# The inverse root of a recurrence's norm: from ScalarE's Sqrt to Newton steps on VectorE

## The chip, the cores and the metric

The kernel runs on one core of one Trainium2 chip. The core has five engines, each of which executes its own instructions in order: TensorE (PE in the profile), VectorE (DVE), ScalarE (ACT), GpSimd (POOL) and SyncE (SP), which here issues nearly all DMAs. They wait for each other by semaphores. The metric is the device time of one execution in microseconds (us): the median of several runs. One execution more is taken by the hardware profiler.

## What is computed

One decoder block over 1024 tokens of width 1024, all in float32. What matters here is the first half, the mixer:

```python
proj = x @ w_in                      # q | f | i | o_gate | pool_v | gate_a | gate_b
f = lb + (1 - lb) * sigmoid(f_pre);  k = 1 - f
o = hgrn2_chunked(silu(q) * 128 ** -0.5, k, i_val, log(f))   # 8 heads, state 128 x 128
o = o * lax.rsqrt(jnp.mean(jnp.square(o), axis=-1, keepdims=True) + RMS_EPS)
o = o * hgrn_norm_g * sigmoid(o_gate)
merged = sigmoid(gate_a) * (o @ w_a) + sigmoid(gate_b) * pooled_branch
mix = merged @ w_out
```

After it come two layer norms and a squared-ReLU MLP (1024 to 4096 to 1024). The line with rsqrt, the inverse root of each head's mean square, is what the change touches.

## The kernel before

Precision. Products of float32 are made of three passes: both operands are split into a high part (a cast on ScalarE, line 118 for weights, line 123 for activations) and a low part (a subtraction on VectorE, lines 119 and 124), and TensorE multiplies high by high, high by low and low by high (lines 201, 203, 204 in prod; 105 to 107 in mm3). The big products go by a seven-product scheme over 2 x 2 blocks: the function pair makes one such set for 256 columns of a weight, with sums of weight blocks on VectorE (lines 241, 284, 289), copies out of PSUM on ScalarE (271) and sums out of PSUM on VectorE (275).

Stages. First the transposes of x and the values i; then the heads, about 150 to 600 us of the span; then the products with w_a, with w_out, the first norm, the MLP and the last norm. Only the heads matter below.

The heads. A loop over eight heads h and two halves u of 512 tokens calls hgrn(h, u), sixteen times in all. It works on one head's 128 channels as 128 x 512 tiles, and each call in this order:

- VectorE scans the products of f (811), ScalarE makes k = 1 - f (813), VectorE takes four reciprocals of 128 columns (817), GpSimd makes small decay tables (819 to 838), VectorE and ScalarE make the scaled queries and keys (841 to 865);
- TensorE transposes the scaled keys, ke (870), ScalarE copies them into the tile tH (872), TensorE multiplies them with the values (875), and VectorE carries the state st over four chunks of 128 tokens (880, 883);
- TensorE makes the scores in the PSUM tile sc (887, 898), and VectorE copies them under the causal mask into the tile att (905), of which there is one only;
- TensorE makes the output o in PSUM, four chunks of one or two matmuls (915, 918);
- ScalarE squares o and sums along each row into ss, 128 x 4 (923); then comes the inverse root (924, 925); then ScalarE copies o, scaled by it, into tH (928), which has one buffer and is thus the tile that the next call's keys will need;
- TensorE transposes it (931), VectorE multiplies with the gain and the output gate in the tile og, two buffers (932), and SyncE stores the row to DRAM (933).

Between the calls stand products that do not depend on the recurrence: the next head's q and f (head_inputs), output gates, the pooling branch (pooled), the gates a and b (gates), and near the end pool_products, which loads rows back into the tiles og and v and splits them for TensorE. o_sums(kp) loads four stored rows of the recurrence back from DRAM, forms sums for the w_a products on VectorE (608 to 611) and stores them (613).

Order. The program is written in the order of the loops, but the framework schedules it: it simulates the program with its own durations, takes for each engine the next instruction that its model has ready, earlier-written ones first, and writes down the order that results. On the chip each engine keeps to that order. A change in one place can so move instructions on all engines. Tiles come from pools with a fixed number of buffers, and a new tile waits until the old use of its buffer is over.

ScalarE's functions sit in tables. Square, Copy, Identity and Sigmoid go with the table that the heads use, Sqrt is in another: in each call line 924 is preceded by a table load, and the next Sigmoid (lines 653, 660, 679, 696) by one back.

Of the kernel before, what the change touches and what calls it, by code (L numbers as in the profile page):

```python
# [9 lines left out]
F32 = mybir.dt.float32  # L10
F32R = mybir.dt.float32r
U32 = mybir.dt.uint32
AF = mybir.ActivationFunctionType
ALU = mybir.AluOpType

_TC = dict(schedule_with_timeline_sim=True)
P = 128
# [6 lines left out]
CH = HALF // P  # L24
# [12 lines left out]
LN_EPS = 1e-5  # L37
RMS_EPS = 1e-6
QSCALE = float(P) ** -0.5
PSUM = bass.MemoryType.PSUM  # L40


@with_exitstack
def tile_hybrid_block(
# [19 lines left out]
    V, A, G, PE = nc.vector, nc.scalar, nc.gpsimd, nc.tensor  # L64
# [5 lines left out]
    const = ctx.enter_context(tc.tile_pool(name="const", bufs=1))  # L70
    pp = ctx.enter_context(tc.tile_pool(name="pp", bufs=4, space=PSUM))
    hd = ctx.enter_context(tc.tile_pool(name="hd", bufs=1, space=bass.MemoryType.DRAM))
# [8 lines left out]
    def nm(s):  # L81
        seq[0] += 1
        return f"{s}_{seq[0]}"
# [48 lines left out]
        out=cmask, in_=cmask, compare_op=ALU.is_ge, fill=0.0, base=0,  # L132
        pattern=[[1, P]], channel_multiplier=-1,
    )
    eps_rms = const.tile([P, 1], F32, name="eps_rms")
    G.memset(eps_rms, RMS_EPS)
    eps_ln = const.tile([P, 1], F32, name="eps_ln")
    G.memset(eps_ln, LN_EPS)
    inv_n = const.tile([P, HALO], F32, name="inv_n")
# [120 lines left out]
    def c_late():  # L260
        return c_tile(False)
# [140 lines left out]
    with tc.tile_pool(name="xr", bufs=8, side="right", reuse_waits="tile") as xr:  # L402
# [17 lines left out]
        V.tensor_sub(e01[:, 8:16], prm[:, 8:16], lb)  # L420
        A.activation(e01, e01, AF.Exp)
        V.tensor_add(lb, e01[:, 0:8], e01[:, 8:16])
# [169 lines left out]
    def loaded(src, tile_of):  # L592
        t = tile_of()
        nc.sync.dma_start(out=t, in_=src)
        return t
# [22 lines left out]
    with tc.tile_pool(name="tmp", bufs=1, side="right", reuse_waits="tile") as tmp:  # L618
# [14 lines left out]
        def tt(tag, dtype=F32):  # L633
            pool = tmp if tag in ("q", "f", "og", "v") else hgp
            return pool.tile([P, HALF], dtype, tag=tag, name=nm(tag), bufs=RINGS.get(tag, 1))

        def small(tag, shape, bufs=2):
            n = math.prod(shape[1:])
            t = hgp.tile([P, max(n, LINE)], F32, tag=tag, name=nm(tag), bufs=bufs)[:, :n]
            return t if len(shape) == 2 else t.rearrange("p (a b) -> p a b", b=shape[2])  # L640


        def head_inputs(h, behind=()):
# [6 lines left out]
            def take_f(u):  # L650
                def take(src):
                    t = fs[u] = fs[u] or tt("f")
                    A.activation(t, src, AF.Sigmoid)
                    A.activation(t, t, AF.Identity, bias=lb[:, h : h + 1], scale=one_lb[:, h : h + 1])
                return take

            def take_q(u):
                def take(src):
                    t = qs[u] = tt("q")
                    A.activation(t, src, AF.Sigmoid)  # L660
                    V.scalar_tensor_tensor(t, src, QSCALE, t, ALU.mult, ALU.mult)
                return take
# [11 lines left out]
        def output_gates(h):  # L674

            def take(dst, src=False):
                def put(t):
                    s = c_late() if src else t
                    A.activation(s, t, AF.Sigmoid)
                    nc.sync.dma_start(out=dst, in_=s)  # L680
# [7 lines left out]
        def gates(j):  # L688
# [3 lines left out]
            def take(dst, src=None, more=None):  # L692
                def put(t):
                    s = (tt("v") if spare else c_late()) if src else t
                    more_of = loaded(more, lambda: tt("v")) if more is not None else None
                    A.activation(s, t, AF.Sigmoid)
                    if more_of is not None:
# [34 lines left out]
        def pooled(g):  # L732
# [58 lines left out]
                (lambda: room(0, 0), lambda: room(0, 1), lambda: room(1, 1)), (take_11, take_12, take_21, lambda _: None),  # L791
            ))

        def blk(t):
            return t.rearrange("p (b s) -> p b s", s=SUB)

# [9 lines left out]
        def hgrn(h, u, ft, q, v, og, state):  # L806
# [8 lines left out]
            for i in range(CH):  # L815
                w = slice(i * P, (i + 1) * P)
                V.reciprocal(r[:, w], fd[:, w])  # L817
            T = small("T", [P, NB])
            G.tensor_copy(T, blk(fd)[:, :, SUB - 1])
            T2 = T.rearrange("p (b e) -> p b e", e=2)  # L820
            p32 = small("p32", [P, CH, 4])
# [21 lines left out]
            V.tensor_mul(kc, k, r)  # L843
            kr = tt("tE")
            V.tensor_mul(blk(kr), blk(kc), bc(T, [P, NB, SUB]))
            A.copy(pairs_of(kc)[:, :, 0], pairs_of(kr)[:, :, 0])
            qc = tt("tF")
# [49 lines left out]
            for c in range(CH):  # L897
# [7 lines left out]
            V.copy_predicated(  # L905
                at, cmask.bitcast(U32).unsqueeze(1).to_broadcast([P, CH, P]),
                sc.rearrange("p (c t) -> p c t", t=P),
# [11 lines left out]
            ss = small("ss", [P, CH])  # L919
            on = tt("tH")  # L920
            for c in range(CH):
                w = slice(c * P, (c + 1) * P)
                A.activation(on[:, w], o[:, w], AF.Square, accum_out=ss[:, c : c + 1])
            A.activation(ss, ss, AF.Sqrt, bias=eps_rms, scale=1.0 / P)
            V.reciprocal(ss, ss)
            for c in range(CH):
                w = slice(c * P, (c + 1) * P)
                A.activation(on[:, w], o[:, w], AF.Copy, scale=ss[:, c : c + 1])
# [18 lines left out]
        for h in range(HEADS):  # L947
            fs, qs = nxt
            state = None
            for u in range(2):  # L950
                v, og = values(h, u), loaded(ogd[h][u], lambda: tt("og"))
                with tc.high_priority(PRIO_LAST) if (h, u) == (HEADS - 1, 1) else nullcontext():
                    state = hgrn(h, u, fs[u], qs[u], v, og, state)
                    if (h, u) == (HEADS - 1, 1):
                        tags = iter(("tD", "tE", "tF", "tC"))
                        o_sums(h - CH, lambda: tt(next(tags)))
                if h + 1 < HEADS and u:
                    nxt = head_inputs(h + 1)
                    if h % 2:
                        output_gates(h + 1)  # L960
                for what, j in EXTRAS.get((h, u), ()):
                    dict(gates=gates, pooled=pooled, pool_products=pool_products, o_sums=o_sums)[what](j)
# [439 lines left out]
```

## Time and profile before

| | us |
|---|---|
| median of 3 runs | 1464.81 |
| lowest and highest run | 1462.62 to 1467.08 |
| the profiled execution, its own time | 1460.19 |
| its span, first to last instruction | 1458.5 |
| TensorE idle within the span | 22.1 |
| of it between 550 and 600 us | 6.75 |
| mean granted clock of TensorE | 0.996 |

How the views are read. A group row reads: line, engine, operation, output tile <- input tiles, shapes, count | busy time, mean duration in ns of one | idle time of the engine just before them, and what ended it. A timeline row reads: start, duration, engine, line, operation, tiles, count, and in brackets the idle time before it with what released it. A row of the view by stretch reads: from and to, then the length of the stretch and the busy time with counts for PE, PEld (weight loads), DVE, ACT and POOL, the granted clock, the busy share of the DMA engines and what they moved. A DMA row gives size and the median time from issue to landing. Numbers of buffers are left out of the names.

### The profile page before, as it was taken

To read this page: it belongs to the slowest core of one execution; us is meant where nothing else is said; L and a number is where in the kernel's file an instruction comes from. 1 tells how busy PE (TensorE), PEld (TensorE's weight loads), DVE (VectorE), ACT (ScalarE), POOL (GpSimd) and SP (SyncE) were. 2 spreads that over 40 slices of the span, in tenths; PEclk is the share of its full clock that TensorE was granted. 3 is DMA by queue.
4 is the path that set the end of the run, shared out by engine and by line. 5 is a ranking of instruction groups with operands and counts; after the bars stand their busy time and mean duration, and the time that the engine had idled before them with its cause. 6 is when DMAs were issued, how large, how long until landed. Compare 5 with 4: busy or idle time off the path is not lost.

```text
span 1458.5 us, 20662 instructions
## 1 busy us (share of the span) xinstructions
PE 1436.4 (98%) x7377; PEld 1187.9 (81%) x7377; DVE 1141.6 (78%) x1838; ACT 758.3 (52%) x1383; POOL 58.6 (4%) x244
## 2 busy tenths in 40 slices
PE   8999999999999998999999999999999999999997
PEld 7888888888888886788888878888888888888886
DVE  5967989899898885768985597666666787777977
ACT  5445565666656655556542376555555443333535
POOL 0001001001000010000002100000000100000000
PEclk9999999999999999999999999999999999999999
DMA  7232233323234447897672225444474874445322
GB/s 253 70 126 87 85 98 101 109 75 114 90 99 138 152 132 249 301 299 241 223 247 99 73 94 195 159 146 144 152 261 149 275 260 150 153 141 163 130 73 116
DMA packets 160615, 226.82 MB, mean 156 GB/s; under 512 B 11232, under 2 KB 84480, under 8 KB 160512
## 3 DMA queue, kind: packets, MB, share of 16 engines
q1 hardware_dynamic: 158576, 218.93, 44.7%
q0 software_dynamic: 1152, 4.19, 0.8%
q10 hardware_dynamic: 784, 2.38, 0.5%
q8 instruction: 58, 0.95, 0.3%
q14 instruction: 45, 0.37, 0.1%
HBM read 154.16 MB, written 71.30 MB: 155 GB/s over the span
## 4 chain that ended last, share of the span: by engine, by line
PE 94%; DVE 3%; DMA 1%; ACT 1%; issue 0%; SPq 0%; DVEq 0%
PE ps_pj L201 16%; PE ps_pj L203 16%; PE ps_pj L204 16%; PE ps_pj L1283 4%; PE ps_pj L1285 4%; PE ps_pj L1284 4%; PE ps_pj L106 3%; PE ps_pj L107 3%; PE ps_pj L105 2%; PE ps_tr L1285 1%; PE ps_tr L1283 1%; PE ps_tr L1284 1%; PE ps_sc L201 1%; PE ps_sc L203 1%; PE ps_sc L204 1%; PE ps_hg L203 1%
## 5 line engine op out<-in xcount | busy, mean ns | idle before, releaser
L201 PE MATMUL ps_pj<-act,w 128*128 128x512 f32 x1068 | 421.6, 395 | 0.4 <-ACT act L123 0.2
L203 PE MATMUL ps_pj<-act,w 128*128 128x512 f32 x1068 | 415.1, 390 | 0.5 <-DVE act L124 0.5
L204 PE MATMUL ps_pj<-act,w 128*128 128x512 f32 x1068 | 414.1, 390 | 0.0
L201 PEld LDWEIGHTS ps_pj<-act,w 128*128 128x128 f32 x1068 | 200.6, 188 | 42.8 <-ACT act L123 0.6
L204 PEld LDWEIGHTS ps_pj<-act,w 128*128 128x128 f32 x1068 | 200.5, 188 | 42.3
L203 PEld LDWEIGHTS ps_pj<-act,w 128*128 128x128 f32 x1068 | 200.6, 188 | 40.6 <-DVE act L124 0.9
L118 ACT CAST w<-t 128x512 fp32r<-128x512 f32 x170 | 104.7, 620 | 105.0 <-PE ps_pj L203 53.8
L118 ACT CAST w<-raw 128x512 fp32r<-128x512 f32 x143 | 88.2, 620 | 117.3 <-PE ps_pj L203 62.5
L119 DVE TENSOR_TENSOR w<-raw,w 128x512 fp32r<-128x512 f32 x143 | 99.8, 702 | 55.2 <-ACT w L118 53.9
L119 DVE TENSOR_TENSOR w<-t,w 128x512 fp32r<-128x512 f32 x170 | 115.9, 685 | 29.6 <-ACT w L118 29.4
L1245 ACT CAST act<-act 128x1024 fp32r<-128x1024 f32 x66 | 66.9, 1050 | 107.9 <-issue 35.0
L1246 DVE TENSOR_TENSOR act<-act,act 128x1024 fp32r<-128x1024 f32 x66 | 79.3, 1220 | 18.5 <-ACT act L1245 15.8
L1285 PE MATMUL ps_pj<-act,act 128*128 128x512 f32 x240 | 92.9, 389 | 0.0
L1284 PE MATMUL ps_pj<-act,act 128*128 128x512 f32 x240 | 92.9, 389 | 0.0
L1283 PE MATMUL ps_pj<-act,act 128*128 128x512 f32 x240 | 92.4, 389 | 0.0
L275 DVE TENSOR_TENSOR c<-c,ps_pj 128x512 f32<-128x512 f32 x95 | 64.5, 681 | 18.0 <-PE ps_pj L204 13.4
L271 ACT COPY c<-ps_pj 128x512 f32<-128x512 f32 x96 | 55.2, 582 | 12.8 <-PE ps_pj L204 12.8
L817 DVE RECIPROCAL tC<-tA 128x128 f32<-128x128 f32 x64 | 54.1, 904 | 0.0
L1284 PEld LDWEIGHTS ps_pj<-act,act 128*128 128x128 f32 x240 | 45.1, 188 | 9.4
L1285 PEld LDWEIGHTS ps_pj<-act,act 128*128 128x128 f32 x240 | 45.1, 188 | 9.4
L1283 PEld LDWEIGHTS ps_pj<-act,act 128*128 128x128 f32 x240 | 45.1, 188 | 9.3
L241 DVE TENSOR_TENSOR t<-raw,raw 128x512 f32<-128x512 f32 x43 | 29.6, 689 | 21.9 <-DMA raw<-in_w_in_dram 19.7
(415 smaller groups left out, 2719.8 us busy)
## 6 DMA issues: line engine op xcount, KB each, us to landing
h<-c SPq DMA_DIRECT2D x106, 256.0 KB, 2.1
act<-h SPq DMA_DIRECT2D x78, 256.0 KB, 2.9
raw<-in_w_in_dram SPq DMA_DIRECT2D x64, 256.0 KB, 3.4
draw<-in_w_down_dram SPq DMA_DIRECT2D x16, 1024.0 KB, 7.8
raw<-in_w_up_dram SPq DMA_DIRECT2D x30, 512.0 KB, 4.2
raw<-in_w_in_dram SPq DMA_DIRECT2D x18, 512.0 KB, 4.0
hf<-h SPq DMA_DIRECT2D x34, 256.0 KB, 2.9
c<-o SPq DMA_DIRECT2D x24, 256.0 KB, 3.4
```

What stands on the lines that cost most here:

```text
L118: A.copy(hi, src)
L119: V.tensor_sub(lo, src, f(hi))
L201: PE.matmul(ps, wh[:, k], th, start=first and k == 0, stop=False, skip_group_check=True)
L203: PE.matmul(ps, wh[:, k], tl, start=False, stop=False, skip_group_check=True)
L204: PE.matmul(ps, wl[:, k], th, start=False, stop=k == CH - 1, skip_group_check=True)
L271: A.copy(t, ps)
L275: V.tensor_add(t, t, ps)
L1245: A.copy(hi, src)
L1246: V.tensor_sub(lo, src, f(hi))
L1283: PE.matmul(ps, hh[:, w], wh, start=fresh and n == 0, stop=False, skip_group_check=True)
L1284: PE.matmul(ps, hh[:, w], wl, start=False, stop=False, skip_group_check=True)
L1285: PE.matmul(ps, hl[:, w], wh, start=False, stop=n == M - 1, skip_group_check=True)
```

## The change

The Sqrt on ScalarE and the reciprocal on VectorE give way to a function of eleven VectorE instructions on 128 x 4 tiles. It forms x = total / 128 + eps, takes a first guess y from the bits of x (as int32: -0.5 times the bits plus a constant), and refines it three times by y = y (1.5 - 0.5 x y y). Three tile names of two buffers each are new, the constant tile eps_rms goes. Line numbers behind the new function are eleven higher in the changed kernel.

```diff
+I32 = mybir.dt.int32
...
+ROOT_GUESS = float(0x5F3759DF)
+ROOT_STEPS = 3
...
-    eps_rms = const.tile([P, 1], F32, name="eps_rms")
-    G.memset(eps_rms, RMS_EPS)
...
+        def inverse_root(total):
+
+            x, y, z = (small(tag, [P, CH]) for tag in ("rx", "ry", "rz"))
+            V.tensor_scalar(x, total, 1.0 / P, RMS_EPS, ALU.mult, ALU.add)
+            V.tensor_scalar(y.bitcast(I32), x.bitcast(I32), -0.5, ROOT_GUESS, ALU.mult, ALU.add)
+            for _ in range(ROOT_STEPS):
+                V.tensor_mul(z, y, y)
+                V.scalar_tensor_tensor(z, z, -0.5, x, ALU.mult, ALU.mult)
+                V.scalar_tensor_tensor(y, z, 1.5, y, ALU.add, ALU.mult)
+            return y
...
-            A.activation(ss, ss, AF.Sqrt, bias=eps_rms, scale=1.0 / P)
-            V.reciprocal(ss, ss)
+            ss = inverse_root(ss)
```

## The prediction

> **What bounds the kernel now.** I read the page's totals, then its chain of waits, then busy time by stretch, then the timeline where TensorE stands.
>
> ```profile
> PE 1436.4 (98%) x7377; PEld 1187.9 (81%) x7377; DVE 1141.6 (78%) x1838; ACT 758.3 (52%) x1383; POOL 58.6 (4%) x244
> PE 94%; DVE 3%; DMA 1%; ACT 1%; issue 0%; SPq 0%; DVEq 0%
> core 0: us, PE busy (x) PEld busy (x) DVE busy (x) ACT busy (x) POOL busy (x), PEclk, DMA share, GB/s
> 160.00:250.00 90.00, 90.00 (x590) 74.74 (x589) 82.84 (x162) 55.06 (x133) 8.66 (x48) 1.00 0.31 98
> 250.00:350.00 100.00, 100.00 (x639) 83.46 (x638) 93.92 (x195) 60.22 (x133) 6.62 (x41) 1.00 0.30 98
> 350.00:450.00 100.00, 100.00 (x680) 82.62 (x679) 89.67 (x182) 58.62 (x130) 5.93 (x37) 1.00 0.34 106
> 450.00:550.00 100.00, 100.00 (x646) 83.40 (x645) 85.45 (x153) 63.16 (x144) 7.93 (x44) 1.00 0.43 137
> 550.00:600.00 50.00, 43.25 (x252) 34.83 (x252) 28.76 (x52) 24.34 (x57) 0.00 (x0) 0.93 0.77 254
> 1000.00:1100.00 100.00, 100.00 (x443) 82.84 (x442) 61.23 (x93) 55.59 (x94) 0.00 (x0) 1.00 0.57 198
> ```
>
> TensorE is the bound. In the heads (160 to 550 us) it never stands; VectorE is busy 351.9 of those 390 us, so 38 are free there; ScalarE has a third to spare. The last row prices a 512-column matmul: 100 / 443 = 0.226 us. TensorE loses 6.7 us in 550 to 600, where the recurrence of the last head ends:
>
> ```profile
> 576.14 0.49 PE L915 MATMUL ps_hg<-v,att 128*128 128x128 f32 x2 [1.21 <-DVE st L883]
> 582.85 1.22 PE L105 MATMUL ps_pj<-w,q 128*128 128x512 f32 x2 [4.66 <-ACT w L118]
> 590.97 0.50 PE L106 MATMUL ps_pj<-w,q 128*128 128x512 f32 x1 [0.84 <-DVE w L119]
> 580.00:585.00 5.00, 2.11 (x5) 1.15 (x5) 1.62 (x4) 2.79 (x5) 0.00 (x0) 0.68 0.94 329
> 585.00:590.00 5.00, 5.00 (x16) 3.67 (x16) 2.48 (x4) 3.75 (x9) 0.00 (x0) 0.64 0.38 115
> ```
>
> The granted clock fell to 0.68 and 0.64 after the 4.66 us gap. It was about half from 582.9 to 588.3, so some 2.7 us of work were lost on top of the wait.
>
> **What is removed.** I number the 16 calls of hgrn as units: unit 2h+u is head h, half u.
>
> ```profile
> L924 ACT ACT_TABLE_LOAD x16 | 20.5, 1283 | 0.3
> L924 ACT ACTIVATE ss<-ss,eps_rms 128x4 f32<-128x4 f32 x16 | 4.8, 298 | 0.2
> L928 ACT ACTIVATE tH<-ps_hg,ss 128x128 f32<-128x128 f32 x64 | 18.2, 366 | 3.7 <-DVE ss L925 3.7
> 162.59 1.28 ACT L924 ACT_TABLE_LOAD   x1
> 163.88 0.30 ACT L924 ACTIVATE ss<-ss,eps_rms 128x4 f32<-128x4 f32 x1
> ```
>
> The built programs hold 35 table loads before and 3 after, since the load back to Sigmoid falls too: 32 x 1.283 = 41.1 us and 16 x 0.298 = 4.8 us leave ScalarE. That engine holds TensorE up only in the 4.66 us, and there the cast came late for its data, ahead of the table load:
>
> ```profile
> 582.18 0.62 ACT L118 CAST w<-og 128x512 fp32r<-128x512 f32 x1 [2.75 <-DMA og<-po]
> 582.81 1.28 ACT L924 ACT_TABLE_LOAD   x1
> ```
>
> So I count the removal at nothing; its upper bound is the whole of that place, 6.7 + 2.7 us. The Trainium skill, "ScalarE: Activation LUTs", section "What ACT_TABLE_LOAD costs", adds a drain of about 1.38 us to each load. The trace starts the next instruction 1.29 us after the load and shows none; by the page 85 us would leave ScalarE instead of 41, hidden either way.
>
> **What is added.** Eleven VectorE instructions of 128x4 per unit, each waiting for the one before, in place of one. Int32 ones are not in the trace. The nearest rows give the price when other work stands between them (start to start 0.07 to 0.08 us) and when one waits directly on the last (0.20):
>
> ```profile
> 8.52 0.17 DVE L418 TENSOR_TENSOR lb<-prm 128x8 f32<-128x8 f32 x1
> 8.72 0.17 DVE L419 TENSOR_TENSOR e<-prm,lb 128x8 f32<-128x8 f32 x1
> 177.10 0.15 DVE L749 TENSOR_TENSOR pA<-pA,inv_n 128x1 f32<-128x1 f32 x1
> 177.17 0.42 DVE L751 SCALAR_TENSOR_TENSOR c<-pA,c 128x255 f32<-128x255 f32 x1
> 177.50 0.69 DVE L284 TENSOR_TENSOR t<-t,raw 128x512 f32<-128x512 f32 x1
> 178.10 0.15 DVE L750 TENSOR_TENSOR c<-pA,c 128x1 f32<-128x1 f32 x1
> ```
>
> VectorE's load thus grows by 16 x (11 - 1) x 0.08 = 13 us, at most 16 x 11 x 0.20 = 35: it fits in the 38 free. The load is not the point. These last rows show what is: two dependent small instructions with two larger ones between them stand 1.00 us apart. The changed program does this ten times over per unit: in its VectorE order 12 to 43 other instructions stand between first and last step of an inverse root in units 0 to 13. What queues behind a step is the rest of VectorE's work, the low halves of line 119 and the sums of line 275 among it, which TensorE and the next unit wait for; but only steps that follow each other directly make it wait, 0.20 each. The memset that falls and the six small tiles I count at nothing: GpSimd is 4% busy, and nothing waits for that memset.
>
> **What is moved.** The root holds up line 928's copies, the transposes of line 931, then the next unit's ke copy (the one tile tH), its state and line 915. Hence the order written by the scheduler changes everywhere up to the products with w_a, and not after. In units 0 to 5 it puts 23 to 31 us of products between line 918's last matmul and line 931, and these cover the root. By unit 6 it has run out of products: TensorE, which executes in order, meets line 931 early.
>
> I price this by windows. Line 905 of unit n+1 overwrites the one att tile, so it starts when line 918 of unit n ends; everything VectorE has between it and the end of root n must run before line 931 can. The prices, start to start:
>
> ```profile
> 160.48 1.27 DVE L811 TENSOR_TENSOR_SCAN tA<-starts,f 128x256 f32<-128x256 f32 x2 [0.78 <-PE ps_hg L918]
> 162.25 0.74 DVE L905 COPY_PREDICATED att<-cmask,sc 128x512 f32<-128x512 uint32 x1
> 162.88 3.37 DVE L817 RECIPROCAL tC<-tA 128x128 f32<-128x128 f32 x4
> 166.18 0.62 DVE L841 TENSOR_TENSOR q<-q,tA 128x512 f32<-128x512 f32 x1
> 166.72 0.16 DVE L925 RECIPROCAL ss<-ss 128x4 f32<-128x4 f32 x1
> 168.58 0.68 DVE L119 TENSOR_TENSOR w<-raw,w 128x512 fp32r<-128x512 f32 x1
> 169.18 0.41 DVE L849 TENSOR_TENSOR tF<-q,tC 128x256 f32<-128x256 f32 x1
> 169.52 0.42 DVE L853 TENSOR_TENSOR q<-q,T 128x256 f32<-128x256 f32 x1
> 170.81 0.28 DVE L858 TENSOR_TENSOR q<-q,p 128x128 f32<-128x128 f32 x1
> 171.01 0.68 DVE L863 TENSOR_TENSOR tA<-q,eq 128x512 f32<-128x512 f32 x1
> ```
>
> That is 1.2 for two scans (1.27 with the tail of the second), 0.63 for line 905, 0.82 for each reciprocal, 0.54 for line 841, 0.60 for 512 columns, 0.34 for 256, 0.20 for 128. Unit 8: line 905 0.63, two scans 1.2, four reciprocals 3.28, line 841 0.55, seven of 512 columns 4.2, three of 256 1.0, two of 128 0.4, five root steps under cover 0.4, six back to back 1.2: 12.9 us with the semaphores, and 0.4 until the first copy of line 928 (366 ns in the row above) is there. TensorE has 24 matmuls (5.4) and 16 scores (0.5), so it stands 12.9 + 0.4 - 5.9 = 7.4 us. The same sum, VectorE against TensorE: unit 6 12.1 / 8.4, late 4.1; unit 7 16.3 / 16.8, on time; unit 9 14.5 / 12.1, late 2.8; unit 10 15.7 / 11.2, late 4.9; unit 11 15.1 / 12.1, late 3.4; unit 12 16.4 / 9.4, late 7.4; unit 13 11.0 / 1.3 (unit 15's scores wait in it too), late 10.2. Together 40.2 us. For the order before the change the same sum gives no lateness in any unit, as the trace has it.
>
> **The end of the heads.** In the changed order o_sums(2) stands on VectorE ahead of unit 15's line 905 and unit 14's root, and its line 608 reads unit 13's result back from DRAM.
>
> ```profile
> o<-og SPq DMA_DIRECT2D x16, 256.0 KB, 2.1
> c<-o SPq DMA_DIRECT2D x24, 256.0 KB, 3.4
> og<-po SPq DMA_DIRECT2D x8, 256.0 KB, 3.9
> ```
>
> From unit 13's transposes: line 932 0.85, store 2.1, two issues and load 4.0, three sums 1.8, line 905 0.6, line 611 0.6, eleven steps 2.2, copy 0.5: 12.8 us, against some 4.0 until line 918 of unit 14 ends: 8.8 late. Behind units 8, 11, 13 and 14 no product covers the ke copy and the state (line 883 alone cost 1.21 before): 1.7 each, 6.8. The first pool product needs tile og, free when unit 14's row is stored: line 932, store, load 3.9, cast 0.6, some 8.9 against 4.0: 4.9; its second half 2.5.
>
> **Sum.** 40.2 + 8.8 + 6.8 + 4.9 + 2.5 = 63.2, less the 6.7 before: +56.5 us. Six of the stalls are as long as the 4.66 us one; at 2.7 each 16, a third of it under the next stall: 11, less the 2.7 before: +8. So +65 on the profiled execution's own 1460.2 us: 1525. That execution lies 4.6 below the median; I forecast 1527. The Trainium skill, "TensorE: Matmul & The Clock Gate", section "Part 1: The HAM clock gate", has the clock halve after an idle window of about 3.4 us and stay so for a busy one: 1.7 lost per stall, +5 in place of +8, and it speaks against this change; the trace had 5.4 us at half.
>
> Bounds: if VectorE's windows (97.7 us in the seven late units) run 10% shorter, no clock is lost and the reloads hide, -28; if waits inside the windows add 7%, ke waits double and no clock loss hides, +21. Own range 1499 to 1548, chance 0.66; beyond it, by waits that add up, 0.03.
>
> **Rivals.** *Only the end is exposed*, 0.20: the middle units come late on VectorE, but TensorE gets there no sooner, because casts or weights hold its products. For it: line 119 waits for casts in many places. Against: 390 us of TensorE without a gap. 10.2 + 8.8 + 3.4 + 7.4 - 6.7, and clock 5: +28, 1490. *All hidden*, 0.07: the 13 us go into the 38 free; 1460 to 1465. For it is the busy share, against it the order. *Faster*, 0.04: ScalarE without table loads lets TensorE through the end of the heads, decided if unit 14's row is stored as early as now; the whole 9.4 us back, 1451. Against it: the wait there was for a DMA, and the changed order stores later. That a table load stays is no case: the built program has three.
>
> **How the numbers follow.** Likeliest 1527. The range 1474 to 1550 takes in the only-the-end case; hidden, faster and the far tail, some 0.2, stay out. 0.3% (4.4 us) is what a measurement can tell: faster 0.05, same 0.06, slower 0.89.
>
> **What would show it.** TensorE idle in the heads of some 60 us, put down to ScalarE's line-928 copies ahead of the transposes of units 6 to 14; first and last root step 7 to 22 us apart; granted clock under 1 in several stretches before the pool products; VectorE waiting for a DMA at o_sums; no difference behind the first w_a products. TensorE at 100% through the heads would make it wrong, and so would root steps 0.2 us apart throughout.

## The result, and the profile after

| | before | after |
|---|---|---|
| median, us | 1464.82 (1462.62 to 1467.08, 4 runs) | 1567.16 (1564.21 to 1571.14, 4 runs) |
| span of the profiled execution, us | 1458.5 | 1564.8 |
| TensorE busy, us | 1436.4 | 1485.6 |
| TensorE idle in the span, us | 22.1 | 79.2 |
| mean granted clock of TensorE | 0.996 | 0.979 |

The changed kernel is slower: ratio 1.070, 95% interval 1.0671 to 1.0730. That is 102 us, where 62 were forecast, and 17 us above the upper end of the range. Of the 106.3 us between the two spans, 57.1 are TensorE idle (+56.5 was forecast), and 49.2 are TensorE busy for longer with the same 7377 matmuls (+8 was forecast for that). The second part is what went wrong.

The totals of the page of after:

```profile
PE 1485.6 (95%) x7377; PEld 1202.7 (77%) x7377; DVE 1166.3 (75%) x1998; ACT 717.5 (46%) x1335; POOL 57.1 (4%) x243
PE 86%; DVE 7%; DMA 4%; ACT 1%; issue 1%; SPq 0%; DVEq 0%; ACTq 0%
```

VectorE gained 24.7 us, between the 13 and the 35 worked out, and ScalarE lost 40.8, where 45.9 were worked out. In the chain of waits VectorE's share rose from 3% to 7%, that of DMAs from 1% to 4%. The busy time by stretch of after shows where TensorE stands, and one thing besides:

```profile
350.00:450.00 100.00, 92.42 (x570) 74.11 (x569) 81.59 (x189) 43.19 (x101) 4.02 (x26) 0.98 0.28 87
450.00:550.00 100.00, 80.75 (x521) 63.35 (x519) 74.11 (x158) 42.24 (x108) 7.58 (x46) 0.96 0.31 95
600.00:650.00 50.00, 30.55 (x245) 24.93 (x246) 32.28 (x77) 16.47 (x50) 3.76 (x20) 0.84 0.44 145
650.00:700.00 50.00, 40.74 (x173) 33.01 (x173) 27.99 (x64) 18.58 (x50) 0.00 (x0) 0.78 0.60 196
1000.00:1100.00 100.00, 100.00 (x431) 80.59 (x430) 61.04 (x93) 54.76 (x93) 0.00 (x0) 1.00 0.43 145
1300.00:1400.00 100.00, 100.00 (x443) 82.86 (x442) 76.39 (x84) 35.21 (x36) 0.00 (x0) 1.00 0.45 145
```

The added idle time lies between 350 and 700 us, with the clock under 1, as forecast. But the row from 1000 to 1100, far behind the heads, where TensorE is always busy at full clock, holds 431 matmuls and had 443 before. These are the products of activation tiles with weight tiles w. The count takes in the matmuls that reach over the ends of the stretch; from start to start, fifteen matmuls apart, the timelines of before and after show it more exactly:

```profile
1050.04 0.39 PE L201 MATMUL ps_pj<-act,w 128*128 128x512 f32 x1
1053.44 0.39 PE L201 MATMUL ps_sc<-act,w 128*128 128x512 f32 x1
```

```profile
1050.02 0.40 PE L202 MATMUL ps_pj<-act,w 128*128 128x512 f32 x1
1053.52 0.40 PE L202 MATMUL ps_pj<-act,w 128*128 128x512 f32 x1
```

A matmul now follows the last after 3.50 / 15 = 0.2333 us instead of 3.40 / 15 = 0.2267. From 1300 on, in the down products of two activation tiles, the count is 443 (442 before). Neither the order nor the clock explains that.

The timeline of one root on VectorE shows the chain as forecast, in a stretch where TensorE still hides it:

```profile
302.41 0.17 DVE L798 TENSOR_SCALAR rx<-ss 128x4 f32<-128x4 f32 x1
302.48 3.38 DVE L829 RECIPROCAL tC<-tA 128x128 f32<-128x128 f32 x4
305.78 0.63 DVE L853 TENSOR_TENSOR q<-q,tA 128x512 f32<-128x512 f32 x1
306.32 0.42 DVE L745 TENSOR_TENSOR pA<-pC 128x265 f32<-128x265 f32 x1
306.66 0.17 DVE L799 TENSOR_SCALAR ry<-rx 128x4 int32<-128x4 int32 x1
...
323.61 0.16 DVE L803 SCALAR_TENSOR_TENSOR ry<-rz,ry 128x4 f32<-128x4 f32 x1
```

Eleven instructions of some 0.16 us stand over 21.2 us. While this root waits, TensorE takes products as filler. The view by stretch for the transposes behind the root alone (four a call, on TensorE) shows the debt that this builds up, first before (line 931), then after (line 942):

```profile
100.00:350.00 250.00, 4.57 (x28) 1.00 0.30 94
350.00:550.00 200.00, 4.52 (x28) 1.00 0.38 122
550.00:700.00 150.00, 1.83 (x8) 0.98 0.84 280
```

```profile
100.00:350.00 250.00, 2.56 (x16) 1.00 0.29 91
350.00:550.00 200.00, 5.30 (x24) 0.97 0.30 91
550.00:700.00 150.00, 5.88 (x24) 0.84 0.45 147
```

Up to 350 us TensorE was as busy as before, but it has finished four calls (16 transposes) instead of seven: the rest was products. Behind 550 us six calls are left instead of two, and too few products to put between them. What TensorE then waits for, by the view of waits of after:

```profile
PE ps_pj L202 <- ACT c L272: 13.6, 6, 8.0
PE ps_hg L927 <- DVE st L895: 9.1, 6, 2.1
PE sc L899 <- ACT tD L858: 8.1, 1, 8.1
PE ps_pj L202 <- ACT f L654: 6.0, 1, 6.0
PE ps_tr L942 <- ACT tH L939: 5.8, 3, 4.5
PE ps_pj L202 <- DVE c L276: 4.4, 1, 4.4
PE ps_pj L202 <- DVE f L276: 3.8, 1, 3.8
PE ps_hg L887 <- ACT tH L884: 2.8, 5, 0.7
```

(Columns: total, times, longest, in us.) Only 5.8 us stand directly before the transposes, line 942 now. Most stand one step further on: at products whose PSUM bank has not been emptied, because its copy or sum waits for VectorE, and once at scores. The two longest waits, in the timeline of after, a selection of the rows of TensorE, VectorE and ScalarE:

```profile
609.31 0.69 DVE L609 TENSOR_TENSOR c<-c,c 128x512 f32<-128x512 f32 x1 [1.96 <-DMA c<-o]
...
610.52 1.74 DVE L829 RECIPROCAL tC<-tA 128x128 f32<-128x128 f32 x2
...
615.67 0.69 DVE L611 TENSOR_TENSOR c<-c,c 128x512 f32<-128x512 f32 x1
...
616.39 0.58 ACT L272 COPY c<-ps_pj 128x512 f32<-128x512 f32 x1 [0.86 <-DVE c L611]
...
617.03 0.80 PE L202 MATMUL ps_pj<-act,w 128*128 128x512 f32 x1 [8.01 <-ACT c L272]
...
645.24 0.69 DVE L857 TENSOR_TENSOR tE<-tD,T 128x512 f32<-128x512 f32 x1
...
645.96 0.41 ACT L858 COPY tD<-tE 128x256 f32<-128x256 f32 x1 [0.30 <-DVE tE L857]
...
646.42 0.65 PE L899 MATMUL sc<-tF,tD 128*32 128x32 f32 x32 [8.08 <-ACT tD L858]
...
649.52 0.48 PE L942 MATMUL ps_tr<-ident,tH 128*128 128x128 f32 x1 [0.56 <-ACT tH L939]
```

The first begins with the o_sums wait for a DMA that the prediction named (1.96 us); the rest of it is VectorE's other work that stands between lines 609 and 611. It blocks a product, by way of a buffer of c that o_sums still uses. In the second the transposes, only 0.56 us late, come behind scores that stood 8.08 us.

### The profile page after: what moved, and what is told of

Same layout as the page of the kernel before. It is cut to its first block, busy times and chain, and to the rows that moved or that the text cites. A ratio compares the mean times of both kernels' runs of the same rounds, so it can differ in the third digit from the quotient of the medians.

```text
span 1564.8 us, 20810 instructions
## 1 busy us (share of the span) xinstructions
PE 1485.6 (95%) x7377; PEld 1202.7 (77%) x7377; DVE 1166.3 (75%) x1998; ACT 717.5 (46%) x1335; POOL 57.1 (4%) x243
## 4 chain that ended last, share of the span: by engine, by line
PE 86%; DVE 7%; DMA 4%; ACT 1%; issue 1%; SPq 0%; DVEq 0%; ACTq 0%
PE ps_pj L202 15%; PE ps_pj L204 15%; PE ps_pj L205 15%; PE ps_pj L1295 4%; PE ps_pj L1294 4%; PE ps_pj L1296 4%; PE ps_pj L108 2%; PE ps_pj L109 2%; PE ps_pj L110 2%; DVE tC L829 2%; PE ps_tr L1295 1%; PE ps_tr L1296 1%; PE ps_tr L1294 1%; PE ps_sc L202 1%; PE ps_sc L204 1%; PE ps_sc L205 1%
## 5 line engine op out<-in xcount | busy, mean ns | idle before, releaser
L202 PE MATMUL ps_pj<-act,w 128*128 128x512 f32 x1068 | 431.5, 405 | 34.3 <-ACT c L272 13.6
L205 PE MATMUL ps_pj<-act,w 128*128 128x512 f32 x1068 | 424.1, 400 | 2.6 <-DVE w L122 2.6
L204 PE MATMUL ps_pj<-act,w 128*128 128x512 f32 x1068 | 424.8, 399 | 0.5 <-DVE act L127 0.5
L202 PEld LDWEIGHTS ps_pj<-act,w 128*128 128x128 f32 x1068 | 203.2, 190 | 87.5 <-ACT c L272 15.2
L205 PEld LDWEIGHTS ps_pj<-act,w 128*128 128x128 f32 x1068 | 203.2, 190 | 52.1 <-DVE w L122 3.5
L204 PEld LDWEIGHTS ps_pj<-act,w 128*128 128x128 f32 x1068 | 203.3, 190 | 47.3 <-DVE act L127 1.1
L1257 DVE TENSOR_TENSOR act<-act,act 128x1024 fp32r<-128x1024 f32 x66 | 79.3, 1221 | 18.9 <-ACT act L1256 18.9
```

Of the source, the lines that this page charges most:

```text
L202: PE.matmul(ps, wh[:, k], th, start=first and k == 0, stop=False, skip_group_check=True)
L204: PE.matmul(ps, wh[:, k], tl, start=False, stop=False, skip_group_check=True)
L205: PE.matmul(ps, wl[:, k], th, start=False, stop=k == CH - 1, skip_group_check=True)
L1257: V.tensor_sub(lo, src, f(hi))
```

## The experiments

Four theories stood at the start, and the expectations speak of them. A: the order costs some 75 us, by the dependent chain on VectorE, and the fall of eps_rms costs the rest, some 27 us, since it moves every later tile of the left side 32 bytes a partition lower. (Tiles are placed from two sides of the memory; the weights w lie on the right side, the activation tiles on the left.) B: order and clock alone, the tiles' places cost nothing. C: the chain's length in itself costs, on whichever engine it runs. D: any root on VectorE in place of ScalarE's Sqrt costs. The kernel before was run beside each; its medians were 1461.8 to 1463.4 us.

**1. The changed kernel with eps_rms kept**: same order, tiles where they were before.

```diff
+    eps_rms = const.tile([P, 1], F32, name="eps_rms")
+    G.memset(eps_rms, RMS_EPS)
```

> The changed kernel with the constant tile eps_rms kept (and its memset), unread. Its instruction order on TensorE and VectorE is that of the changed kernel; its tiles lie where those of the kernel before lie, 32 bytes higher. Theory A (two causes: the order, and the 32 bytes by which the missing tile moved every tile behind it): matmuls follow each other at 0.227 us instead of 0.2325 in full stretches of the first 1250 us, some 27 us less, so about 1540 us (1533 to 1548), with TensorE idle as in the changed kernel, some 79 us. Theory B (order and clock alone, the place of the tiles does nothing): 1567 us as the changed kernel, 0.2325 us between matmuls.

1546.26 us (1544.03 to 1548.11), ratio 1.0569 (1.0552 to 1.0585). So 20.9 us of the loss go with 32 bytes that nothing reads (27 were expected), and 83.7 stay against the kernel before run beside this one (1462.6). TensorE's idle time is 77.7 us, as in after. The view by stretch shows 443 matmuls from 1000 to 1100 us again, and the heads as in after:

```profile
450.00:550.00 100.00, 81.16 (x506) 65.30 (x505) 76.36 (x167) 42.48 (x110) 7.69 (x47) 0.90 0.30 95
1000.00:1100.00 100.00, 100.00 (x443) 82.81 (x442) 62.72 (x95) 55.58 (x94) 0.00 (x0) 1.00 0.45 150
```

**2. The kernel before with its two eps constants in one tile**: the shift alone, no change of order.

```diff
-    eps_rms = const.tile([P, 1], F32, name="eps_rms")
+    eps = const.tile([P, 2], F32, name="eps_ln")
+    eps_ln, eps_rms = eps[:, 0:1], eps[:, 1:2]
...
-    eps_ln = const.tile([P, 1], F32, name="eps_ln")
```

> The kernel before, its two eps constants in one tile, so that every tile behind lies 32 bytes lower, as in the changed kernel; Sqrt and its table loads stay, and the order is that of the kernel before. Theory A: matmuls at 0.2325 us, about 1492 us (1485 to 1500), TensorE idle still some 22 us. Theory B: 1465 us as before.

1483.18 us (1481.97 to 1484.67), ratio 1.0138 (1.0123 to 1.0154): +20.6 us, a little under the lower end expected of A. B falls. The order is that of before, and the view by stretch has the 431 matmuls of after:

```profile
1000.00:1100.00 100.00, 100.00 (x431) 80.55 (x430) 60.70 (x92) 54.66 (x94) 0.00 (x0) 1.00 0.45 153
```

By the totals of the two pages TensorE is busy 1460.8 us instead of 1436.4, so the shift costs 24.4 us of its time: 17.8 in the 3204 products of lines 201, 203 and 204 (their three group rows together 1268.6 against 1250.8), the rest for the most part in nearly a thousand other products of activation tiles with weights. The profiled execution was idle 2.0 us less than that of before, so that the spans differ by 22.4.

**3. The Newton steps on GpSimd**, eps_rms kept. Only the guess stays on VectorE; a step takes four GpSimd instructions, and the chain has 14 instructions.

```diff
-            V.tensor_scalar(x, total, 1.0 / P, RMS_EPS, ALU.mult, ALU.add)
+            G.tensor_scalar(x, total, 1.0 / P, RMS_EPS, ALU.mult, ALU.add)
...
-                V.tensor_mul(z, y, y)
-                V.scalar_tensor_tensor(z, z, -0.5, x, ALU.mult, ALU.mult)
-                V.scalar_tensor_tensor(y, z, 1.5, y, ALU.add, ALU.mult)
+                G.tensor_mul(z, y, y)
+                G.tensor_mul(z, z, x)
+                G.tensor_scalar(z, z, -0.5, 1.5, ALU.mult, ALU.add)
+                G.tensor_mul(y, z, y)
```

> [...] Theory A: the steps no longer stand in VectorE's queue between large instructions, the order has products to cover every unit but the last two, and these are late by 5 us together: 1462 to 1480 us. Rival C (the longer chain itself is the cost, wherever it runs): still above 1510.

1480.78 us (1479.51 to 1481.48), ratio 1.0121 (1.0105 to 1.0136), just over the upper end. C falls: the chain has more instructions and each takes longer, and the loss is 18 us, not 84. The timeline of this run shows the difference:

```profile
288.86 0.43 POOL L800 TENSOR_SCALAR rx<-ss 128x4 f32<-128x4 f32 x1 [15.96 <-ACT tH L938]
...
292.69 0.11 DVE L801 TENSOR_SCALAR ry<-rx 128x4 int32<-128x4 int32 x1
292.95 0.20 POOL L803 TENSOR_TENSOR rz<-ry 128x4 f32<-128x4 f32 x1
...
297.28 0.26 POOL L806 TENSOR_TENSOR ry<-rz,ry 128x4 f32<-128x4 f32 x1
```

Twelve Newton instructions take 4.6 us, 0.28 apart for the most part; the one step that goes to VectorE costs nearly 4 us from x to y. On an engine with little else to do (GpSimd is busy 9% of the span here), the chain stays together: by the timelines the sixteen roots take 4.3 to 10.7 us from first to last instruction, in after 2.1 to 23.1. What loss remains is at the end of the heads: TensorE is busy 34.4 of the 50 us between 550 and 600, at a clock of 0.74; before it was 43.25, at 0.93.

**4. No Newton step**, eps_rms kept: two VectorE instructions, the bit guess alone. The refinement is left out.

```diff
-ROOT_STEPS = 3
+ROOT_STEPS = 0
```

> The changed kernel with eps_rms kept and no Newton step: scale and first guess only, two VectorE instructions, no table load; it leaves out the refinement. Theory A: the order is late by 1.5 us in all: 1460 to 1472 us. It also prices the table loads alone: if they were worth something, it is below the 1465 of the kernel before. Rival D (the table loads' place in the order was what kept products between the units, any root on VectorE loses them): above 1490.

1471.63 us (1470.96 to 1473.84), ratio 1.0064 (1.0047 to 1.0081). The 32 table loads are gone here too, and with a chain hardly longer than the one removed the time is not under that of before. So D falls, and no gain from the table loads shows. This run has an order of its own, though, and TensorE is idle 9.7 us more than before; a gain smaller than what this order costs isn't excluded.

**5. The kernel before with ten more VectorE instructions for each root**, independent and read by nobody.

```diff
+            for n in range(10):
+                V.tensor_scalar(small(f"ld{n % 3}", [P, CH]), dec, 1.0 / P, RMS_EPS, ALU.mult, ALU.add)
```

> The kernel before, with ten more VectorE instructions of 128x4 behind each root, each on its own and read by nobody (they compute nothing of the output). VectorE gets as many small instructions as the change gives it, but no chain. If the length of the dependent chain is what costs (A), the order hardly moves and the time stays within 1463 to 1475 us, TensorE idle 22 to 30 us. If VectorE's mere load is what costs, all of it or most: 1515 to 1550.

1465.11 us, ratio 1.0018 (1.0006 to 1.0030). 160 more instructions on VectorE, as many as the change adds, cost 2.3 us. As they follow each other 0.07 us apart they add 9.4 us to its busy time (1151.0 against 1141.6), not the 24.7 of the change; but in proportion to the busy time 24.7 us would cost 6 (an estimate) and not 84. So most of the loss is not VectorE's load. That the instructions wait for each other is what is left, and experiments 4 and 6 vary it.

**6. One Newton step** (ROOT_STEPS = 1), eps_rms kept; two of the three refinements are left out.

> The changed root with one Newton step in place of three (it leaves out two steps of the refinement), small tiles where they were before: a chain of five VectorE instructions. If the cost grows with the chain (A), it lies between no step (1471.6) and three steps (1546.3): my windows give 27 us of lateness, with the clock it makes 1500 to 1515 us. If it is the leaving of ScalarE's table function or any root on VectorE that costs, as near to 1472 as no step: 1468 to 1480.

1504.41 us (1503.10 to 1506.17), ratio 1.0277 (1.0260 to 1.0295). With chains of two, five and eleven instructions (experiments 4, 6 and 1) the loss against before is 9.0, 41.6 and 83.7 us: 32.6 / 3 = 10.9 us for each link from two to five, 42.1 / 6 = 7.0 from five to eleven. It grows with the chain, and D's 1468 to 1480 is missed.

**7 to 11. Which tile's place, and against what.** All have the kernel before's instructions in its order (in experiment 7 one early matmul and one early copy stand a few places off), and differ only in padding that nobody reads and its memsets; experiment 8 has the edit of experiment 2 as well. A tile of one column takes 32 bytes a partition, which experiments 8 and 12 bear out: 8 columns of 4 bytes on the other side undo it. The edits, one a run:

```diff
--- 7: activation tiles (and constants ahead of them) 32 bytes higher, the others of the left side 64
+    gap = ctx.enter_context(tc.tile_pool(name="gap", bufs=1))
+    G.memset(gap.tile([P, 8], F32, name="gap1"), 0.0)
...
+    G.memset(const.tile([P, 1], F32, name="gap0"), 0.0)
--- 8: edit of experiment 2, and the right side, with the weights w, 32 bytes lower
-    G.memset(pad.tile([P, 24], F32, name="pad_top"), 0.0)
+    G.memset(pad.tile([P, 32], F32, name="pad_top"), 0.0)
--- 9: the right side alone 32 bytes lower (the two lines above)
--- 10: the left side 64 bytes higher (11: range(4), 128 bytes)
+    for n in range(2):
+        G.memset(const.tile([P, 1], F32, name=f"gap{n}"), 0.0)
```

> The kernel before with only the activation tiles moved by 32 bytes a partition (one column of padding ahead of them, the other tiles on 64-byte places). Order of before. If the place of the moving operand of the products is what costs: 512-column matmuls 0.233 us apart and 1480 to 1486 us, as with all tiles moved. If it is another of the moved tiles (the heads' small tiles, constants, stores): 0.2277 apart and 1460 to 1468 us.

> The kernel before with the tiles of the left side 32 bytes lower, as the change puts them, and the tiles of the right side (the weights w among them) moved by 32 bytes too, so that the two operands of a product stand to each other as before. Order of before. If only the distance of the two operands modulo 64 bytes matters: 0.2277 us from matmul to matmul and 1460 to 1468 us. If the moving operand's own place matters: 0.233 and 1480 to 1488; if each operand's place matters by itself, more than 1488.

> The kernel before with only the right side's tiles (the weights w among them) moved by 32 bytes; the activation tiles stay where they were. Order of before. If the distance of the two operands modulo 64 bytes matters: 512-column matmuls 0.233 us apart and 1480 to 1488 us, although no activation tile moved. If the moving operand's own place had been the cause and the right side's move only a cure for it: 0.2277 and 1460 to 1468 us.

> The kernel before with all tiles of the left side 64 bytes higher; the right side stays. Order of before. If the distance modulo 64 bytes matters, this changes nothing: 0.2277 us apart, 1460 to 1468 us. If any change of the distance from that of before costs (a larger period): 0.233 and 1480 to 1488.

> The kernel before with all tiles of the left side 128 bytes higher; the right side stays. Order of before. A move by 64 bytes had cost 8.8 us and put the 512-column matmuls 0.2295 us apart. If the distance of the two operands counts modulo 128 bytes: 0.2277 us and 1460 to 1468 us. If every 32-byte place that leaves the distance of before costs by a larger period: 0.2295 or more and 1470 to 1485.

| | distance of act and w against before | ratio, 95% interval | median, us | matmuls from 1000 to 1100 us |
|---|---|---|---|---|
| 2 | act 32 lower | 1.0138 (1.0123 to 1.0154) | 1483.18 | 431 |
| 7 | act 32 higher | 1.0139 (1.0124 to 1.0155) | 1483.34 | 430 |
| 8 | both 32 lower | 1.0003 (0.9993 to 1.0012) | 1463.34 | 443 |
| 9 | w and the right side 32 lower | 1.0138 (1.0123 to 1.0154) | 1482.82 | 430 |
| 10 | act 64 higher | 1.0057 (1.0040 to 1.0074) | 1471.73 | 439 |
| 11 | act 128 higher | 1.0127 (1.0111 to 1.0144) | 1480.72 | 432 |

Moving the right side alone (9) costs as much as moving the activations alone (7), and moving both costs nothing (8). So it is the distance between the places of the two operands, not the place of one. The rule that I had for it, modulo 64 bytes, is refuted by 10 and 11: 64 bytes cost 8.8 us (neither of the two outcomes expected) and 128 cost 18.9. (Where the expectations put the matmuls of before 0.2277 us apart, the timeline has 0.2267.) The views by stretch of experiments 8, 9 and 10, in this order:

```profile
1000.00:1100.00 100.00, 100.00 (x443) 82.80 (x442) 63.09 (x96) 56.46 (x96) 0.00 (x0) 1.00 0.57 196
```

```profile
1000.00:1100.00 100.00, 100.00 (x430) 80.33 (x429) 60.24 (x92) 54.42 (x93) 0.00 (x0) 1.00 0.44 148
```

```profile
1000.00:1100.00 100.00, 100.00 (x439) 82.04 (x438) 62.49 (x95) 55.88 (x95) 0.00 (x0) 1.00 0.51 177
```

The count of matmuls and the time of weight loads (PEld, 82.8 against 80.3) fall together; in these stretches the clock is full and TensorE never idle.

**12. The changed kernel with the distance restored**: nothing but the right side 32 bytes lower; eps_rms stays away.

```diff
-    G.memset(pad.tile([P, 24], F32, name="pad_top"), 0.0)
+    G.memset(pad.tile([P, 32], F32, name="pad_top"), 0.0)
```

> The changed kernel, complete, with nothing else than the right side's tiles moved 32 bytes lower too, so that the distance of the two operands is again that of the kernel before; no tile added, the same instructions in the same order. If the distance accounts for the part of the loss that is not order: 512-column matmuls 0.2277 us apart and 1542 to 1551 us, as with the constant kept. If it is the missing constant or its memset: 1562 to 1572 us as the changed kernel.

1546.88 us (1544.56 to 1548.01), ratio 1.0571 (1.0548 to 1.0593). The same as experiment 1: in the changed kernel too it is the distance, not the missing constant or its memset. No version of the change was faster than the kernel before.

## Why the prediction was wrong

**The bound and the direction.** Right: TensorE bounds, it has no slack, and the change opens waits in the second half of the heads.

**The removal, counted at nothing.** Right: experiment 4 has no table loads in the heads and is 9.0 us slower than before, not faster (its order differs too, as said there).

**VectorE's load.** Forecast 13 us, at most 35; measured 24.7, and it is not what costs most (experiment 5).

**The waits, +56.5 us.** Right in sum: +57.1 in after and +55.6 in experiment 1. Partly wrong in place. The terms for the transposes and for o_sums, 49.0 us, were to stand before line 931 (942). The view of waits has 5.8 there, and 8.1 at the scores and some 35 at products (line 202 in the page of after); that sum is near the forecast. The lateness on VectorE was there, but it reached TensorE earlier in its queue, at products and scores whose copies and sums stand in the same queues of VectorE and ScalarE. The ke copies and the state were put at 6.8, and the two rows are 9.1 and 2.8, of which 1.2 was there before. The reload of tile og was put at 4.9 and its second half at 2.5; no product at line 108 waits for more than 0.9. That the whole comes out within 1 us is thus in part luck. Slips in the sum itself (10.2 for 10.1, 12.8 for 12.7, and 2 us added for the 4.6 between the profiled execution and the median) change little. The rival that only the end is exposed is refuted by 19.3 us of idle time between 450 and 550 us.

**The clock, +8 us.** The mechanism was right, the size too small by a factor of two to three. Counted in stretches of 5 us, as TensorE's busy time times the part of the clock that was withheld, the loss is 20.0 us in after and 2.5 before: +17.5. In experiments 1 and 12 it is +23.0 and +18.4. I priced six stalls one by one and took a third off for those that follow on another. There were 18 waits of over 1 us between 350 and 700 us, and the clock fell in six places there. Five of them cost 1.6 to 3.0 us each, near the 2.7 of the forecast; the last, where the stalls stand close together, cost more and not less. The view by stretch of after, TensorE alone, with one of the five ahead of it:

```profile
435.00:440.00 5.00, 4.89 (x14) 0.66 0.01 2
...
635.00:640.00 5.00, 3.34 (x23) 1.00 0.65 224
640.00:645.00 5.00, 0.00 (x0) 0.63 0.14 40
645.00:650.00 5.00, 2.82 (x58) 0.50 0.48 125
650.00:655.00 5.00, 3.56 (x15) 0.50 0.41 137
655.00:660.00 5.00, 3.35 (x14) 0.50 0.43 159
660.00:665.00 5.00, 1.38 (x7) 0.50 0.66 209
665.00:670.00 5.00, 3.22 (x13) 0.50 0.27 93
670.00:675.00 5.00, 5.00 (x24) 0.80 0.39 121
```

After the wait of 8.08 us the clock stays at half for 25 us, through 14 us of work, and rises only in the first five microseconds without a gap: 8.2 us lost in one place. The Trainium skill, "TensorE: Matmul & The Clock Gate", section "Part 1: The HAM clock gate", has full clock come back after a busy window of some 3.4 us. These rows agree with it; what fell short was to apply it to each stall by itself, at 1.7 us or at 2.7.

**Busy time without a term.** Of TensorE's 49.2 us, some 24 are the shift of the tiles (experiment 2) and 17.5 the clock. Some 7 are left, as are 8 in experiments 1 and 12, where the distance is that of before: 31.2 - 23.0 and 26.3 - 18.4. The forecast had nothing for them. The transposes behind the root are among them (13.7 us in the view above, 10.9 before, the clock included); the others were not followed up.

**The step that failed**: "The memset that falls and the six small tiles I count at nothing: GpSimd is 4% busy, and nothing waits for that memset." I priced the instruction that falls and not the tile. Its 32 bytes a partition moved the activation tiles against the weights, and that put the products of the two 0.2333 us apart instead of 0.2267: 20.6 us alone (experiment 2), 20.9 in the changed kernel (experiment 1), given back when the distance is restored (experiment 12). The sign "no difference behind the first w_a products" failed for the same reason. Without this step the changed kernel takes 1546 to 1547 us, within the range on record, 3 to 4 us under its upper end. The second step that failed is a size: the +8 for the clock, which measured 17.5 to 23, and with the 7 to 8 us above it makes up the rest of the distance to 1527.

What stays open: how the cost depends on the distance between the operands, beyond the four other distances tried, and which access meets which. That the order costs by the debt of recurrence work that it builds up, and not by the root steps' own waits, was read from the traces and is not shown by a run; no run held the chain together on VectorE in an otherwise unchanged order. The placing of the 18 us that remain with the chain on GpSimd was read from one trace as well.

## What to carry to other kernels

A chain of small dependent instructions on a loaded, in-order engine is priced by where the scheduler puts its links, not by their busy time: here 24.7 us of VectorE cost 84, and on an engine with little else to do a chain of 14 cost 18. In a kernel bound by TensorE, price stalls that stand close together as one: here single ones cost 1.6 to 3.0 us of clock each and the cluster 8.2. And before a constant or a small tile is added or removed, see which large tiles move with it; here padding that put the matmul operands back at their old distance gave the loss back.

## What was not expected of the hardware

Matmuls of 512 columns on two 32-bit operands follow each other after 0.2267 us or 0.2333 by the distance between the places of their two operands in a partition, at full clock and with no wait in the trace. Of the distances tried, that of the kernel before was best; 64 bytes off it gave 0.2289, 32 in either direction 0.2333 and 128 gave 0.2324, start to start between 1000 and 1100 us. It shows in no wait, and in the mean of a group only as 400 ns against 395 (line 201, experiment 2); it shows best in the count of matmuls in a stretch where TensorE is always busy.
